# Attention scores of two heads: one product over 128 rows of the array each, or three products over 64 rows side by side

## The chip, the cores and the metric

The kernel runs on one core of a Trainium2 chip. A core has a matrix engine (TensorE; "PE" in the profile, its weight loads "PEld"), a vector engine (VectorE, "DVE"), a scalar engine (ScalarE, "ACT"), a general engine (GpSimd, "POOL") and a queue for transfers (SyncE, "SP"). They run side by side and wait for one another through semaphores. TensorE multiplies a stationary operand, which a weight load puts into the array, by a moving operand that is streamed through it; the result goes to a separate memory of eight banks, which VectorE and ScalarE read.

The metric is device microseconds of one execution, lower is better. Times are medians over several executions; the profile is of one execution, with its own time.

## What is computed

Two sequences (2048 and 512 positions, 1024 channels) go through two layers and a last RMSNorm. The first layer, which the change touches, is windowed attention with 16 query heads of width 64; every four query heads share one of 4 key and value heads:

```python
qb = q.reshape(b, nb, BLOCK, N_KV_HEADS, GROUP, HEAD_DIM)
kw = band_windows(k, nb)            # the block before, the own, the next: 384 keys
scores = jnp.einsum('bnqhgd,bnkhd->bnhgqk', qb, kw) * scale + bias
scores = jnp.where(mask, scores, -jnp.inf)
m = jnp.maximum(jnp.max(scores, axis=-1, keepdims=True), sk)
p = jnp.exp(scores - m)
p = p / (jnp.sum(p, axis=-1, keepdims=True) + jnp.exp(sk - m))
o = jnp.einsum('bnhgqk,bnkhd->bnqhgd', p, vw)
return x + (o * jax.nn.silu(gate)) @ w_out
```

`sk` is a learned logit per head, `bias` a table by distance. The second layer mixes by a two-dimensional Fourier transform, with a gate and an output projection. Everything is float32.

## The kernel before

Float32 accuracy is made of products in a shorter format (`F32R` in the code). An operand is split in two parts, "hi" (rounded) and "lo" (the rest). Most products are made of three products of parts, hi x hi, hi x lo and lo x hi: that is `matmul3` (lines 95 to 97), and each projection in the profile shows up under these three lines.

The attention layer goes through five chunks of 512 positions (`CHUNKS`: the short sequence, then four of the long one). For each chunk the keys and values of the chunk and its neighbours are projected. A key part is kept twice in `kwin`, once in partitions 0 to 63 and once in 64 to 127, for both parts, hi and lo. Then eight pairs `p` of query heads follow, each with four blocks `b` of 128 queries and two heads `j`.

- `qg_proj` projects queries and gates of a pair (128 columns, two heads of 64). Its step `evac_q` (lines 370 to 379) reads the query bank of 128 partitions, of which the first 64 are head 0 and the others head 1, and makes one tile `qab` with two halves: for head 0, hi in partitions 0 to 63 and lo in partitions 64 to 127; for head 1, hi in partitions 64 to 127 and lo in 0 to 63. Two instructions of ScalarE and two of VectorE, of 64 partitions each, do this. The queries are scaled by -1/8, so that a minimum takes the place of the maximum.
- `scores(b, j)` (line 422) makes two products over all 128 rows (line 428): the stationary operand holds hi and lo of the queries one above the other, the moving one the same part of the keys in both halves of the partitions, first hi and then lo. So two products contain all four products of parts. They run over 384 key columns, and over 256 in the first and last block of a sequence. The result stands in one of two banks, `spt`, which take turns. Then the softmax follows: VectorE adds the bias and takes the minimum (line 440), ScalarE takes the exponential with its sum (line 444), VectorE the reciprocal (line 447) and the scaling (line 450, in the first chunk also lines 453 and 456). The tile `S` has `LAG + 2` = 5 buffers.
- `transp(b, j)` transposes the probabilities on TensorE (line 467) and splits them (lines 468 and 469), `av(b)` multiplies them by the values (line 481), `out_evac(b)` adds the parts, applies the gate and splits the result for the output projection `out_proj`.

One loop over `i` sets the order: 64 steps per chunk, one for each pair of heads, block and head (`HB` lists the blocks and heads), and five more to run out. In step `i` come the scores of step `i`, the transposes of step `i - LAG` (`LAG` is 3), half of the step's share of filling work (the projections of the next pair, or the output projection), the value product of the head pair that ended two steps before (`AVLAG`), and the other half of the filling. This order is what the program hands in; a planner then orders the instructions of each engine by their priorities and its own estimate of when operands are ready, unless an order is pinned. `tc.keep_in_program_order(x)` pins `x` behind the instruction that was last handed in on its engine.

One product in the kernel does not use all of the array's rows: the bias table is looked up once at the start by a product of 33 rows and 16 columns (line 245).

Of the kernel before, what the change touches and what calls it, by code (L numbers as in the profile page):

```python
# [8 lines left out]
F32 = mybir.dt.float32  # L9
# [3 lines left out]
AF = mybir.ActivationFunctionType  # L13
ALU = mybir.AluOpType
# [4 lines left out]
P = 128  # L19
# [9 lines left out]
LAG = 3  # L29
# [10 lines left out]
def f32(ap):  # L40
    return ap.bitcast(F32)
# [3 lines left out]
def encoder(  # L45
# [3 lines left out]
    PE, ACT, DVE, POOL, SP = nc.tensor, nc.scalar, nc.vector, nc.gpsimd, nc.sync  # L49
# [85 lines left out]
    def attention_phase():  # L135

        with ExitStack() as es:
# [76 lines left out]
            ps = bank("idle")  # L214
# [40 lines left out]
            spt = []  # L255
# [98 lines left out]
            def qg_proj(c, p, hs, res, invb=None):  # L354

                steps = []
                st = {}

                def load():
                    st["q"] = load_w(c, p, f"q{c}_{p}", None if p else DVE)  # L360
                    st["g"] = load_w(c, 12 + p, f"g{c}_{p}", None if p else DVE)

                def mm(which, k):
                    if k == 0:
                        st["ps" + which] = bank(f"{which}p{c}_{p}")
                    ks = slice(k * P, (k + 1) * P)
                    w = st[which]
                    matmul3(st["ps" + which], (w[0][:, ks], w[1][:, ks]), hs[k], k == 0, k == KD - 1)

                def evac_q():  # L370
                    ps = scaled(st["psq"], invb, f"q{p}")
                    qab = ap.tile([P, 2, CH], F32R, align_bytes=LINE, tag="qab", bufs=2, name=f"qab{c}_{p}")
                    qa, qb = qab[:, 0], qab[:, 1]
                    ACT.activation(qa[0:64], ps[0:64], AF.Copy, scale=-0.125)
                    DVE.scalar_tensor_tensor(qa[64:128], ps[0:64], -0.125, f32(qa[0:64]), ALU.mult, ALU.subtract)
                    ACT.activation(qb[64:128], ps[64:128], AF.Copy, scale=-0.125)
                    DVE.scalar_tensor_tensor(qb[0:64], ps[64:128], -0.125, f32(qb[64:128]), ALU.mult, ALU.subtract)  # L377
                    res["q"] = (qa, qb)

                def evac_g():  # L380
                    ps = scaled(st["psg"], invb, f"g{p}")
                    th = ap.tile([P, CH], F32, tag="tmp", bufs=2, name=f"th{c}_{p}")
                    ACT.activation(th, ps, AF.Tanh, scale=0.5)
                    s = ap.tile([P, CH], F32, tag="s", bufs=2, name=f"s{c}_{p}")
                    DVE.scalar_tensor_tensor(s, th, 1.0, ps, ALU.add, ALU.mult)
                    res["s"] = s

                steps.append(load)
                for k in range(KD):
                    steps.append(lambda k=k: mm("q", k))  # L390
                steps.append(evac_q)
                for k in range(KD):
                    steps.append(lambda k=k: mm("g", k))
                steps.append(evac_g)
                return steps

            def attention(c, p, res, uTs):
# [21 lines left out]
                    k1 = 2 if tok + (b + 1) * P == hi_t else 3  # L419
                    return gb, k0, k1  # L420

                def scores(b, j):
                    gb, k0, k1 = span(b)
                    q = res["q"][j][:, b * P : (b + 1) * P]
                    ps = spt[nS[0] % 2]
                    nS[0] += 1
                    for part in range(2):
                        PE.matmul(  # L428
                            ps[:, 2 + k0 * P : 2 + k1 * P],
                            q,  # L430
                            kwin[g][:, part, b * P + k0 * P : b * P + k1 * P],
                            start=part == 0,
                            stop=part == 1,
                        )

                    e0, e1 = (1 + k0 * P, 386) if k1 == 3 else (0, 1 + k1 * P)
                    n = e1 - e0
                    s = ap.tile([P, 388], F32, tag="S", bufs=LAG + 2, name=f"S{c}_{p}_{b}_{j}")
                    mn, den = s[:, 386:387], s[:, 387:388]
                    DVE.tensor_tensor_reduce(  # L440
                        out=s[:, e0:e1], in0=ps[:, 1 + e0 : 1 + e1], in1=st["bias"][:, j, 386 - e1 : 386 - e0][:, ::-1],
                        scale=1.0, scalar=3.0e38, op0=ALU.add, op1=ALU.min, accum_out=mn,
                    )
                    last_exp[0] = ACT.activation(  # L444
                        s[:, e0:e1], s[:, e0:e1], AF.Exp, bias=mn, scale=-1.0, accum_out=den
                    )
                    DVE.reciprocal(den, den)  # L447
                    ks = slice(1 + k0 * P, 1 + k1 * P)
                    if c:
                        DVE.tensor_scalar(s[:, ks], s[:, ks], den, None, ALU.mult)  # L450
                    elif j:

                        ACT.activation(s[:, ks], s[:, ks], AF.Copy, scale=den)
                    else:

                        DVE.tensor_scalar(s[:, ks], s[:, ks], den, None, ALU.mult, ALU.add, accum_out=mn)
                    st[b, j] = s
# [234 lines left out]
            for c in range(len(CHUNKS)):  # L692

                if c > 1:
                    hs, halo = make_h(c, invb)
                for s in tail:
                    s()
                if c == 1:
                    hs, halo = make_h(c, invb)
                if c:  # L700
                    invb0 = kv_proj(c, hs, halo)
                else:
                    invb0 = kv_proj(c, hs, halo, first_norms, early)
                rowd, sk = bias
                uTs = []
                res = [{} for p in range(8)]
                at = [attention(c, p, res[p], uTs) for p in range(8)]
                for s in qg_proj(c, 0, hs, res[0], invb0):
                    s()
                at[0][0]()  # L710
                fill = []
                for i in range(64 + LAG + AVLAG):
                    p, n = divmod(i, 8)
                    if n == 0 and i < 64:
                        if p < 7:

                            fill = qg_proj(c, p + 1, hs, res[p + 1], invb0)
                            fill.pop(0)()
                            at[p + 1][0]()
                            if i == 0 and c == 0:  # L720

                                for s in fill[:8]:
                                    s()
                                fill = fill[8:]
                        else:
                            op = out_proj(c, uTs)
                            fill, rest, tail = op[:4], op[4:7], op[7:]
                    if c + 1 < len(CHUNKS):
                        if i == 24:
                            norm_steps = stats(c + 1)  # L730
                        if i >= 38 and i % 2 == 0 and norm_steps:
                            inv = norm_steps.pop(0)()
                        elif i == 56:
                            invb = spread(c + 1, inv)
                    if c in EXTRA and i in EXTRA[c]:
                        EXTRA[c][i]()
                    if c == len(CHUNKS) - 1 and i in AHEAD:
                        AHEAD[i]()
                    if c == 0 and i % 8 == 3 and 1 <= p < 3:
                        load_w(0, LATE[p - 1], f"late{p}", late=last_exp[0])  # L740
                    if i < 64:
                        at[p][1](*HB[n])
                    k = i - LAG
                    if 0 <= k < 64:
                        at[k // 8][2](*HB[k % 8])
                    if i < 64:
                        m = len(fill) * (n + 1) // 8 - len(fill) * n // 8
                        todo = fill[len(fill) * n // 8 :][:m]
                        for s in todo[: m // 2]:
                            s()  # L750
                    k -= AVLAG
                    if 0 <= k < 64 and k % 2 == 1:
                        b = k % 8 // 2
                        at[k // 8][3](b)
                        if b % 2 == 1:
                            at[k // 8][4](b)
                    if i < 64:
                        for s in todo[m // 2 :]:
                            s()
                    elif rest:  # L760
                        rest.pop(0)()
# [802 lines left out]
```

## Time and profile before

| what | value |
|---|---|
| median of 3 runs | 1649.08 us (1646.85 to 1652.1) |
| the profiled execution, its time | 1648.75 us |
| its span, first to last instruction | 1647.0 us |
| TensorE busy | 1628.4 us (99%), 8939 matmuls |
| VectorE busy | 1199.0 us (73%) |
| ScalarE busy | 892.7 us (54%) |
| GpSimd busy | 434.5 us (26%) |
| granted TensorE clock, mean | 0.998 |

Matmuls are pipelined: one that follows starts long before the one ahead of it has ended, so the profile's durations of single matmuls overlap. How long a matmul holds the engine is read from the distance between starts, or from the chain in order of time, where each piece lasts until the next. "Busy" counts the time in which at least one is under way. In a group of the profile, "128*128 128x384" says how many rows and columns of the array are used, and how many partitions and elements the result has. The releaser behind an arrow is inferred from semaphores.

### The profile page before, as it was taken

Reading aid. Unit: us, or ns where it says so; the run is one execution under the profiler, and the core shown is the slowest. Engines: PE = TensorE matmul, PEld = TensorE weight load, DVE = VectorE, ACT = ScalarE, POOL = GpSimd, SP = SyncE. Lnnn points to the kernel's source line nnn. Section 1 sums busy time; section 2 is a strip of 40 time slices with the busy share of each in tenths; the row PEclk is TensorE's granted clock in tenths of the full one; section 3 lists DMA queues with packets and bytes.
Section 4 is the critical chain, followed back from the end, with each engine's and each line's share of the span. In section 5 each row is a group of like instructions: output and inputs, shape, how many; then the busy total and the mean of one; then the engine's idle time right before and its main releaser. Section 6 shows DMA issues by size and latency. Waiting matters only on the chain.

```text
span 1647.0 us, 25858 instructions
## 1 busy us (share of the span) xinstructions
PE 1628.4 (99%) x8939; PEld 1401.4 (85%) x8939; DVE 1199.0 (73%) x2844; ACT 892.7 (54%) x2035; POOL 434.5 (26%) x605
## 2 busy tenths in 40 slices
PE   9999999999999999999999999999999999999998
PEld 7887888888898888988888888888888888888886
DVE  6787565888538886478884588858767667988696
ACT  6788644677326675256762466636545454343252
POOL 2454751431404322224214142121111111100010
PEclk9999999999999999999999999999999999999999
DMA  8475886665766555765648765657565469655862
GB/s 303 150 284 213 314 319 225 221 230 186 278 218 227 196 217 182 279 250 160 233 140 312 252 210 187 217 195 249 205 237 185 173 220 391 217 192 191 333 208 90
DMA packets 100637, 374.05 MB, mean 227 GB/s; under 512 B 12139, under 2 KB 22379, under 8 KB 83100
## 3 DMA queue, kind: packets, MB, share of 16 engines
q1 hardware_dynamic: 81708, 297.91, 52.2%
q0 software_dynamic: 16464, 70.30, 11.0%
q10 hardware_dynamic: 2336, 4.20, 0.7%
q8 instruction: 71, 1.16, 0.3%
q14 instruction: 58, 0.48, 0.1%
HBM read 281.10 MB, written 91.26 MB: 226 GB/s over the span
## 4 chain that ended last, share of the span: by engine, by line
PE 82%; DMA 4%; DVE 4%; POOL 3%; ACT 3%; issue 2%; SPq 0%; POOLq 0%; DVEq 0%; ACTq 0%
PE av L481 6%; PE spt L428 6%; PE pt L467 5%; PE qp L95 4%; PE qp L97 4%; PE qp L96 4%; PE op L95 4%; PE gp L95 4%; PE op L97 4%; PE gp L97 4%; PE op L96 4%; PE gp L96 4%; PE W L96 2%; PE W L97 2%; PE W L95 2%
## 5 line engine op out<-in xcount | busy, mean ns | idle before, releaser
L444 ACT ACTIVATE S<-S 128x385 f32<-128x385 f32 (+1 forms) x320 | 190.8, 596 | 63.3 <-DVE S L440 61.5
L469 DVE TENSOR_TENSOR pts<-pt,pts 128x384 fp32r<-128x384 f32 (+1 forms) x320 | 168.4, 526 | 42.0 <-ACT pts L468 39.6
L468 ACT CAST pts<-pt 128x384 fp32r<-128x384 f32 (+1 forms) x320 | 144.0, 452 | 83.4 <-PE pt L467 80.3
L440 DVE CUSTOM_DVE_ANT_0 S<-spt,b 128x385 f32<-128x385 f32 (+1 forms) x320 | 168.4, 527 | 28.2 <-PE spt L428 25.7
L428 PE MATMUL spt<-kwin,qab 128*128 128x384 f32 (+1 forms) x640 | 157.2, 327 | 1.9 <-DVE S L440 1.7
L500 POOL TENSOR_TENSOR o<-o,s 128x256 f32<-128x256 f32 x75 | 55.3, 738 | 375.0 <-DVE o L498 374.9
L467 PE MATMUL pt<-ident,S 128*128 128x128 f32 x896 | 150.7, 273 | 0.0
L428 PEld LDWEIGHTS spt<-kwin,qab 128*128 128x128 f32 x640 | 117.9, 188 | 27.9 <-DVE S L440 3.0
L95 PE MATMUL qp<-h,wq 128*128 128x512 f32 x320 | 137.5, 430 | 2.0 <-ACT wq L116 1.4
L95 PE MATMUL gp<-h,wg 128*128 128x512 f32 x320 | 137.8, 431 | 0.0
L481 PEld LDWEIGHTS av<-pts,v 128*128 128x128 f32 x896 | 126.3, 189 | 12.1 <-DVE qab L377 0.6
L481 PE MATMUL av<-pts,v 128*128 128x256 f32 x896 | 135.8, 285 | 0.3 <-DVE qab L377 0.2
L95 PE MATMUL op<-wo,uT 128*128 128x512 f32 x320 | 126.5, 397 | 1.6 <-ACT invb L173 0.9
L97 PE MATMUL qp<-h,wq 128*128 128x512 f32 x320 | 126.7, 396 | 0.2 <-POOL wq L121 0.2
L467 PEld LDWEIGHTS pt<-ident,S 128*128 128x128 f32 x896 | 113.9, 140 | 15.1 <-DVE pts L469 3.5
L96 PE MATMUL qp<-h,wq 128*128 128x512 f32 x320 | 126.2, 395 | 0.0
L97 PE MATMUL gp<-h,wg 128*128 128x512 f32 x320 | 125.9, 393 | 0.0
L96 PE MATMUL gp<-h,wg 128*128 128x512 f32 x320 | 125.7, 393 | 0.0
L96 PE MATMUL op<-wo,uT 128*128 128x512 f32 x320 | 125.7, 393 | 0.0
L97 PE MATMUL op<-wo,uT 128*128 128x512 f32 x320 | 124.7, 391 | 0.0
L450 DVE TENSOR_SCALAR S<-S 128x384 f32<-128x384 f32 (+1 forms) x256 | 118.7, 464 | 7.9
L447 DVE RECIPROCAL S<-S 128x1 f32<-128x1 f32 x320 | 51.3, 160 | 65.7 <-ACT S L444 62.7
(408 smaller groups left out, 4252.4 us busy)
## 6 DMA issues: line engine op xcount, KB each, us to landing
wo<-wsd SPq DMA_DIRECT2D x32, 1024.0 KB, 5.0
wq<-wsd SPq DMA_DIRECT2D x31, 1024.0 KB, 4.9
wg<-wsd SPq DMA_DIRECT2D x31, 1024.0 KB, 6.8
x<-x1d SPq DMA_DIRECT2D x40, 512.0 KB, 3.9
b<-b21d SPq DMA_DIRECT2D x40, 512.0 KB, 5.4
b<-rowd SPq DMA_DIRECT2D x40, 384.0 KB, 4.3
xs<-in_x_dram SPq DMA_DIRECT2D x23, 512.0 KB, 6.1
s2d<-gt POOLq DMA_DIRECT2D x40, 256.0 KB, 3.9
```

The lines of the kernel that those rows point to most:

```text
L95: PE.matmul(out, a[0], b[0], start=start, stop=False, skip_group_check=more)
L96: PE.matmul(out, a[0], b[1], start=False, stop=False, skip_group_check=more)
L97: PE.matmul(out, a[1], b[0], start=False, stop=stop, skip_group_check=more)
L428: PE.matmul(ps[:, 2 + k0 * P : 2 + k1 * P], q, kwin[g][:, part, b * P + k0 * P : b * P + k1 * P], start=part == 0, stop=part == 1,)
L440: DVE.tensor_tensor_reduce(out=s[:, e0:e1], in0=ps[:, 1 + e0 : 1 + e1], in1=st["bias"][:, j, 386 - e1 : 386 - e0][:, ::-1], scale=1.0, sca ...
L444: last_exp[0] = ACT.activation(s[:, e0:e1], s[:, e0:e1], AF.Exp, bias=mn, scale=-1.0, accum_out=den)
L450: DVE.tensor_scalar(s[:, ks], s[:, ks], den, None, ALU.mult)
L467: PE.transpose(ps[:, kb, :], s[:, 1 + kb * P : 1 + (kb + 1) * P], ident)
L468: ACT.copy(hi[:, k0:k1, j, :], ps[:, k0:k1, :])
L469: DVE.tensor_tensor(lo[:, k0:k1, j, :], ps[:, k0:k1, :], f32(hi[:, k0:k1, j, :]), ALU.subtract)
L481: PE.matmul(out, v, pt[:, kb].rearrange("p h q -> p (h q)"), start=kb == k0 and part == 0, stop=kb == k1 - 1 and part == 1,)
L500: eng.tensor_tensor(o, o, s, ALU.mult)
```

## The change

The queries of both heads now lie in one layout: `qab[:, 0]` holds hi and `qab[:, 1]` lo, each with head 0 in partitions 0 to 63 and head 1 in 64 to 127. One instruction of ScalarE and one of VectorE, of 128 partitions, make them.

`scores(b)` handles both heads of a block. It makes three products of parts per head, hi x hi, hi x lo and lo x hi, each over the 64 partitions of its head, so over 64 rows of the array; lo x lo is left out. The products of head 0 and head 1 alternate, head 0 in bank `spt[0]`, head 1 in `spt[1]`. All six are pinned in the order in which they are handed in. The softmax of both heads (`soft`, the unchanged rest of the old function) follows. In the loop `scores` is called in every other step, for both heads; transposes, value products and filling keep their steps. The buffers of `S` are 5, as before, written as a number.

```diff
                 def evac_q():
                     ps = scaled(st["psq"], invb, f"q{p}")
                     qab = ap.tile([P, 2, CH], F32R, align_bytes=LINE, tag="qab", bufs=2, name=f"qab{c}_{p}")
-                    qa, qb = qab[:, 0], qab[:, 1]
-                    ACT.activation(qa[0:64], ps[0:64], AF.Copy, scale=-0.125)
-                    DVE.scalar_tensor_tensor(qa[64:128], ps[0:64], -0.125, f32(qa[0:64]), ALU.mult, ALU.subtract)
-                    ACT.activation(qb[64:128], ps[64:128], AF.Copy, scale=-0.125)
-                    DVE.scalar_tensor_tensor(qb[0:64], ps[64:128], -0.125, f32(qb[64:128]), ALU.mult, ALU.subtract)
-                    res["q"] = (qa, qb)
+                    ACT.activation(qab[:, 0], ps, AF.Copy, scale=-0.125)
+                    DVE.scalar_tensor_tensor(qab[:, 1], ps, -0.125, f32(qab[:, 0]), ALU.mult, ALU.subtract)
+                    res["q"] = qab
...
-                def scores(b, j):
+                def scores(b):
+
                     gb, k0, k1 = span(b)
-                    q = res["q"][j][:, b * P : (b + 1) * P]
-                    ps = spt[nS[0] % 2]
-                    nS[0] += 1
-                    for part in range(2):
-                        PE.matmul(
-                            ps[:, 2 + k0 * P : 2 + k1 * P],
-                            q,
-                            kwin[g][:, part, b * P + k0 * P : b * P + k1 * P],
-                            start=part == 0,
-                            stop=part == 1,
-                        )
+                    for i, (qp, kp) in enumerate(((0, 0), (0, 1), (1, 0))):
+                        for j in range(2):
+                            rows = slice(64 * j, 64 * j + 64)
+                            tc.keep_in_program_order(PE.matmul(
+                                spt[j][:, 2 + k0 * P : 2 + k1 * P],
+                                res["q"][rows, qp, b * P : (b + 1) * P],
+                                kwin[g][rows, kp, b * P + k0 * P : b * P + k1 * P],
+                                start=i == 0,
+                                stop=i == 2,
+                            ))
+                    for j in range(2):
+                        soft(b, j)
+
+                def soft(b, j):
+                    gb, k0, k1 = span(b)
+                    ps = spt[j]
...
-                    s = ap.tile([P, 388], F32, tag="S", bufs=LAG + 2, name=f"S{c}_{p}_{b}_{j}")
+                    s = ap.tile([P, 388], F32, tag="S", bufs=5, name=f"S{c}_{p}_{b}_{j}")
...
-                    if i < 64:
-                        at[p][1](*HB[n])
+                    if i < 64 and n % 2 == 0:
+                        at[p][1](n // 2)
```

## The prediction

> **What bounds the kernel now.** I read the page first (shares, slices, chain by engine and line), then busy time by stretches, then who waits for whom on PE.
>
> ```profile
> span 1647.0 us, 25858 instructions
> PE 1628.4 (99%) x8939; PEld 1401.4 (85%) x8939; DVE 1199.0 (73%) x2844; ACT 892.7 (54%) x2035; POOL 434.5 (26%) x605
> ...
> PE 82%; DMA 4%; DVE 4%; POOL 3%; ACT 3%; issue 2%; SPq 0%; POOLq 0%; DVEq 0%; ACTq 0%
> PE av L481 6%; PE spt L428 6%; PE pt L467 5%; PE qp L95 4%; PE qp L97 4%; PE qp L96 4%; PE op L95 4%; PE gp L95 4%; PE op L97 4%; PE gp L97 4%; PE op L96 4%; PE gp L96 4%; PE W L96 2%; PE W L97 2%; PE W L95 2%
> ```
>
> TensorE is busy 99% of the span and holds 82% of the chain that ended last; the score products (L428) are 6% of it. A busy PE need not be full, so two stretches of attention come next. Columns are length, then busy time of PE, PEld, DVE, ACT, POOL, the granted clock, DMA share, GB/s.
>
> ```profile
> 254.00:458.00 204.00, 204.00 (x1131) 176.72 (x1130) 150.75 (x436) 115.69 (x296) 61.86 (x77) 1.00 0.64 225
> ...
> 662.00:866.00 204.00, 204.00 (x1173) 179.60 (x1171) 150.67 (x424) 116.34 (x288) 51.52 (x69) 1.00 0.61 212
> PE spt L428 <- DVE S L440: 1.7, 2, 1.4
> ...
> PE av L481 <- DVE qab L377: 0.2, 1, 0.2
>   PEld spt L428: 3.0, 5
> ```
>
> In attention PE has no idle time, at clock 1.00, while VectorE has 53 us of 204 free and ScalarE 88. PE waits for the evaluation of scores 1.7 us in all (plus 3.0 us ahead of weight loads, last row, from the view of L440) and for the queries 0.2 us. So any PE time that the change saves or adds there is the kernel's, and work taken from VectorE or ScalarE is worth almost nothing.
>
> **What a score product costs now.** The chain in order of time gives spacings, not the overlapping durations:
>
> ```profile
> 591.66 0.35 PE spt L428 x2
> 592.01 0.33 PE pt L467 x3
> 592.34 0.23 PE gp L95
> ...
> 596.50 0.35 PE spt L428 x2
> L428 PE MATMUL spt<-kwin,qab 128*128 128x384 f32 x512 | 131.5, 338 | 1.7 <-DVE S L440 1.7
> L428 PE MATMUL spt<-kwin,qab 128*128 128x256 f32 x128 | 25.7, 283 | 0.1
> 48.03 0.64 PE L428 MATMUL spt<-kwin,qab 128*128 128x256 f32 x4
> 48.50 0.40 PE L95 MATMUL gp<-h,wg 128*128 128x512 f32 x1
> ```
>
> Two products over 384 key columns hold PE 0.35 us, 0.175 each. The four over 256 columns run from 48.03 to 48.50, 0.118 each; 512 columns take 0.23. A pair of heads in one block now has four: 512/4 = 128 pairs at 0.70 us and 128/4 = 32 pairs at 0.47, together 104.6 us, the 6% of the chain.
>
> **Products of parts.** Each pair now issues six products in three rounds instead of four in four. No row of this trace shows two products at once in different rows of the array, so the cost is bounded: at best two side by side cost one, three rounds, 0.525 and 0.354 us; at worst six follow one another, 1.05 and 0.708. Against four, that is 128 x -0.175 + 32 x -0.118 = -26.2 us, or 128 x 0.35 + 32 x 0.236 = +52.4. Between lies a limit of weight loads: each product loads its own 128 columns, and loads stand no closer than 0.11 us below. Six in a row take 0.65: less than four products now at 384 columns, more at 256. The likeliest value I take is the best case: the streamed columns set the spacing in the rows above (0.118, 0.175, 0.23 for 256, 384, 512), and two heads stream through different rows.
>
> **The change of array shape.** The six work on 64 rows; what stands ahead and behind works on 128. The trace has one such change, the small bias product (L245: 33 rows by 16 columns, far from 128 x 128), in both directions. PE, then PEld:
>
> ```profile
> 17.25 0.39 PE L96 MATMUL kp<-h,wk 128*128 128x512 f32 x1
> 17.47 0.39 PE L97 MATMUL kp<-h,wk 128*128 128x512 f32 x1
> 17.79 1.03 PE L245 MATMUL bp<-oh,rb 33*16 33x512 f32 x2
> 18.75 0.38 PE L95 MATMUL vp<-wv,h 128*128 128x256 f32 x1
> 18.97 0.28 PE L96 MATMUL vp<-wv,h 128*128 128x256 f32 x1
> 17.25 0.19 PEld L97 LDWEIGHTS kp<-h,wk 128*128 128x128 f32 x1
> 17.79 0.11 PEld L245 LDWEIGHTS bp<-oh,rb 33*16 33x16 f32 x2 [0.35 <-issue]
> 18.75 0.19 PEld L95 LDWEIGHTS vp<-wv,h 128*128 128x128 f32 x1 [0.85 <-ACT xs L155]
> 18.86 0.19 PEld L96 LDWEIGHTS vp<-wv,h 128*128 128x128 f32 x1
> L245 PE MATMUL bp<-oh,rb x2: 589/594/600, 17.8 to 18.2; 33*16 33x512 f32 x2
> ```
>
> Normally a weight load starts with the product before it (17.25 and 17.25). At the change it does not: L97 starts at 17.47, its follower would at 17.70, yet load and product start at 17.79: 0.09 us late, and waiting for nothing shown. The two bias products end at 18.82 together, the second lasts 0.59, so it began at 18.23, 0.44 behind the first; the next could begin at 18.67 and does at 18.75, 0.08 late. Its load too starts only then, and the product behind stands 0.22 away instead of the 0.118 of 256 columns: 0.10 for the exposed load of 128 columns. (The wait for xs named there is no proof of a data wait: the release is inferred.) Into 64 rows I take 0.09 + 0.10, since the new loads have 128 columns; back 0.08 + 0.10: 0.37 us per pair. The Trainium skill (TensorEngine Tiling (Array Packing), Tiling Modes, Key Properties) states that a change of tiling mode drains the TensorE, without a price. The trace shows late starts of 0.09 and 0.08; were a drain the whole tail of a 512-column product, 0.39 - 0.23 = 0.16, the change would be 2 x (0.16 + 0.10) = 0.52 a pair by that rule and the sum below +57 instead of +33, an estimate that lies inside my forecast's own range.
>
> Bounds: at least 0, because scores to transposes changes kind of product without loss (0.35 and 0.33 above are whole spacings), and the bias product is one sample of another type and shape; at most a full latency and a full load each way, 0.39 - 0.23 + 0.19 = 0.35, or 0.70 a pair. Times 160 pairs: 0, 59.2 or 112 us. I take 59.2, from the only row that changes rows.
>
> **Order.** The six are pinned, each behind the PE instruction traced before it, where scores could earlier slip forward into a gap. In attention there is no gap, so I count 0; the wait it could lengthen is the 4.7 us for L440. Queued behind a waiting score product are transposes, projections and value products, all on PE. Both heads now fill both banks at once, and VectorE must read both before the next pair, two steps (591.66 to 596.50, 4.84 us) on. One head's softmax takes:
>
> ```profile
> 603.64 0.55 DVE L440 CUSTOM_DVE_ANT_0 S<-spt,b 128x385 f32<-128x385 f32 x1
> 604.24 0.62 ACT L444 ACTIVATE S<-S 128x385 f32<-128x385 f32 x1
> 604.98 0.16 DVE L447 RECIPROCAL S<-S 128x1 f32<-128x1 f32 x1
> 605.18 0.42 DVE L450 TENSOR_SCALAR S<-S 128x384 f32<-128x384 f32 x1
> 601.21 0.52 PE L428 MATMUL spt<-kwin,qab 128*128 128x384 f32 x2
> ```
>
> Scores begun at 601.21 are read at 603.64 to 604.19, 3.0 us on; a second head's read adds 0.55, to 3.5, or ends 4.94 us on if it stands behind the first head's whole chain (at 605.60). The first leaves 1.3 us of slack, so 0; without that cover 0.1 us on each of 160 pairs, 16 us. The transposes come three steps after the scores (1.5 x 4.84 = 7.3 us) for the first head and four for the second, against chains that end 4.4 and at most 6.4 us after them. Five score tiles remain; the sixth tile needed reuses one whose transposes stand a step earlier, so no new wait.
>
> **Queries.** Per pair of heads and chunk, four evacuations of 64 partitions become two of 128:
>
> ```profile
> L374 ACT ACTIVATE qab<-qp x40: 572/588/593, 38.5 to 1047.2; 64x512 fp32r<-64x512 f32 x40
> L375 DVE SCALAR_TENSOR_TENSOR qab<-qp,qab x40: 683/684/687, 39.1 to 1048.1; 64x512 fp32r<-64x512 f32 x40
> L376 ACT ACTIVATE qab<-qp x40: 592/593/598, 39.8 to 1049.0; 64x512 fp32r<-64x512 f32 x40
> L377 DVE SCALAR_TENSOR_TENSOR qab<-qp,qab x40: 692/693/694, 40.4 to 1049.9; 64x512 fp32r<-64x512 f32 x40
> ```
>
> If 128 partitions take as long as 64, 40 x 0.59 = 23.7 us of ScalarE and 40 x 0.69 = 27.7 of VectorE go, none on the path: PE waits for queries 0.2 us. If the time grows with partitions, nothing goes and nothing is lost. Count 0. DMAs, bias, softmax arithmetic, transposes and value products keep their number.
>
> **Sum.** -26.2 + 59.2 = +33 us. The profiled run took 1648.75 with a span of 1647.0; the median of the runs is 1649.08, 0.3 above. 1648.75 + 33 is about 1682.
>
> **Rivals.** (1) *The change of rows is free* and the heads run side by side: -26.2, so 1622.5; faster. For it: PE is the bound with no idle time, and the change from scores to transposes costs nothing. Against it: the bias product. It decides once a pair loses under 26.2/160 = 0.16 us, less than half of my 0.37. (2) *Weight loads follow one another* and the change of rows costs 0.37: the rounds take six loads, five beyond the first, already paid, then one last stream. At 384 columns 5 x 0.11 + 0.175 = 0.725 + 0.37 against 0.70, +0.395 x 128; at 256, 0.55 + 0.118 + 0.37 against 0.47, +0.568 x 32: +69, so 1717. For it: load rows never overlap by more than their tail. Against: nothing in the rows beyond that the loads shown all use the same rows of the array. The Trainium skill, in the same section, has different tiles load and multiply in parallel, which would exclude (2) and (3); no run here shows it yet. (3) *The heads don't run side by side*, so the change doesn't do what it says: +52.4 + 59.2 = +112, so 1760. No row speaks for or against. (4) *Free change, loads in line*: six at 0.11 against four, 128 x -0.04 + 32 x 0.19 = +1, so about 1650.
>
> **How the numbers follow.** Chances: my forecast 0.43; (1), with a switch under 0.16, 0.20; (2) 0.19; (3) 0.10; (4) 0.08, of which 0.05 within 0.3%, which is about what a measurement can tell from no change. Slower: 0.43 + 0.19 + 0.10 + 0.03 = 0.75; same 0.05; faster 0.20. The range leaves out (3) and the dearest switch, 0.10 to 0.15: from 1620, under (1), to 1728, over (2). The likeliest's own, with 0.25 to 0.52 us a pair for the switch (40 to 83 us), is 1662 to 1706.
>
> **What would show it.** In the profile after: L428-type products in 64 rows, starting in twos within a few hundredths of a us if side by side, rounds 0.175 apart (right) or 0.22 (rival 2) or twice 0.175 (rival 3); a first weight load that starts with its own product rather than with the one before, and the same for the first load behind the six, some 0.37 us a pair (right) or a load already early (rival 1). PE's waits for the score reads should stay under 10 us; more means that the banks are held. VectorE's busy time should fall by up to 28 us without effect. The prediction is wrong if other matmuls slip between the six (each time another change of rows, 0.37), or if the bias product's delay was a data wait.

## The result and the profile after

The changed kernel takes 1675.3 us (median of 4 runs, 1674.4 to 1676.51) against 1648.64 for the kernel before beside it: 1.0157 times as long, 95% interval 1.0143 to 1.0171. That is 26.7 us slower; 33 were forecast.

The first view is the page of the changed kernel: its span, shares and chain by line. L425 are now the score products (L428 before), L470 the transposes, L484 the value products, L443 the reading of the scores.

```profile
span 1673.8 us, 26522 instructions
## 1 busy us (share of the span) xinstructions
PE 1656.0 (99%) x9259; PEld 1353.6 (81%) x9259; DVE 1177.5 (70%) x2804; ACT 874.9 (52%) x1995; POOL 435.2 (26%) x605
...
PE pt L470 6%; PE spt L425 6%; PE av L484 6%; PE qp L95 4%; PE qp L97 4%; PE qp L96 4%; PE op L95 4%; PE gp L95 4%; PE gp L97 4%; PE gp L96 4%; PE op L96 4%; PE op L97 4%; PE fo L97 2%; PE fo L96 2%; PE fo L95 2%
```

TensorE is still busy 99% of the span; the span grew by 26.8 us and TensorE's busy time by 27.6. VectorE does 21.5 us less and ScalarE 17.8, and nobody gained by it. The score products are still 6% of the chain: three rounds in place of four did not make them cheaper. The transposes rose from 5 to 6%.

Next come PE's instructions in order of time around one pair of heads, then PEld's in the same stretch (columns: start, duration of the merged group, engine, line).

```profile
599.89 0.39 PE L96 MATMUL qp<-h,wq 128*128 128x512 f32 x1
600.12 0.40 PE L97 MATMUL qp<-h,wq 128*128 128x512 f32 x1
600.45 0.80 PE L425 MATMUL spt<-kwin,qab 64*128 64x384 f32 x6
601.17 0.55 PE L470 MATMUL pt<-ident,S 128*128 128x128 f32 x3
601.47 0.49 PE L95 MATMUL qp<-h,wq 128*128 128x512 f32 x1
```

```profile
599.89 0.19 PEld L97 LDWEIGHTS qp<-h,wq 128*128 128x128 f32 x1
600.45 0.47 PEld L425 LDWEIGHTS spt<-kwin,qab 64*128 64x128 f32 x6 [0.36 <-DVE o L501]
601.17 0.31 PEld L470 LDWEIGHTS pt<-ident,S 128*128 128x128 f32 x3 [0.25 <-ACT pts L471]
```

Read the distances of the starts. The product ahead holds PE from 600.12 to 600.45, 0.33 us instead of 0.23: 0.10 lost on the way in. The six hold it from 600.45 to 601.17, 0.72 us. Six in line at 0.175 would be 1.05, three rounds 0.525; the rest, 0.20, is the first load, now exposed, and the way out. One by one, the trace has the six starting in twos, 3 to 4 ns apart: at 600.446 and 600.450, 600.729 and 600.732, 600.906 and 600.910. The first round takes 0.28 instead of 0.18, so the exposed load is 0.10; from the last round to the transposes it is 0.26, so the way out is 0.09. The three transposes go from 601.17 to 601.47, 0.30 instead of the 0.24 that stood between 601.57 and 601.81 before (rows of the next fence, kernel before): 0.06 for their exposed load. Both first loads, at 600.45 and at 601.17, start with their own product and not with the one ahead, as a load does otherwise (599.89 and 599.89). The releasers named in the brackets are inferred: the small product of an experiment below has the same delay in a kernel of the old order.

```profile
601.57 0.49 PE L467 MATMUL pt<-ident,S 128*128 128x128 f32 x3
601.81 0.48 PE L95 MATMUL qp<-h,wq 128*128 128x512 f32 x1
```

So a pair at 384 columns loses 0.10 + (0.72 - 0.70) + 0.06 = 0.18 us. A pair at 256 columns, from the same view near the start:

```profile
48.04 0.39 PE L97 MATMUL qp<-h,wq 128*128 128x512 f32 x1
48.36 0.62 PE L425 MATMUL spt<-kwin,qab 64*128 64x256 f32 x6
48.91 0.50 PE L95 MATMUL gp<-h,wg 128*128 128x512 f32 x1
49.25 0.40 PE L96 MATMUL gp<-h,wg 128*128 128x512 f32 x1
```

Here the way in costs 0.09, the six take 0.55 against 0.47, and the 512-column product behind takes 0.34 instead of 0.23. With 0.06 behind where transposes follow, 128 x 0.18 + 32 x 0.23 = 30 us; the measured difference is 26.7. Summed over the whole of both traces, the distances from a start to the next grew by 15.3 us behind products of 512 columns, 8.8 behind transposes and 2.8 behind score products, and by nothing behind the rest together: 26.9. The first two are about what the rows give. The score products should have grown by 128 x 0.02 + 32 x 0.08 = 5.1 us by the rows; most of the 3 to 4 us lies there, since the kernel before has longer pauses between its score products than the changed one. PE's waits for the reading of scores are not the cause of the loss:

```profile
PE spt L425 <- DVE S L443: 1.8, 3, 0.8
```

```profile
  DVE S L443: 5.3, 8
```

The first row is from who waited for whom on PE, the second from the view of L425, for PE and its weight loads together: 5.3 us against 4.7 before.

### The profile page after: what moved, and what is told of

It reads as the page before. It is cut to its first block, busy times and chain, and to the rows that moved or that the text cites. A ratio compares the mean times of both kernels' runs of the same rounds, so it can differ in the third digit from the quotient of the medians.

```text
span 1673.8 us, 26522 instructions
## 1 busy us (share of the span) xinstructions
PE 1656.0 (99%) x9259; PEld 1353.6 (81%) x9259; DVE 1177.5 (70%) x2804; ACT 874.9 (52%) x1995; POOL 435.2 (26%) x605
## 4 chain that ended last, share of the span: by engine, by line
PE 85%; DVE 4%; ACT 3%; DMA 3%; issue 2%; POOL 2%; SPq 0%; DVEq 0%; POOLq 0%; ACTq 0%
PE pt L470 6%; PE spt L425 6%; PE av L484 6%; PE qp L95 4%; PE qp L97 4%; PE qp L96 4%; PE op L95 4%; PE gp L95 4%; PE gp L97 4%; PE gp L96 4%; PE op L96 4%; PE op L97 4%; PE fo L97 2%; PE fo L96 2%; PE fo L95 2%
## 5 line engine op out<-in xcount | busy, mean ns | idle before, releaser
L443 DVE CUSTOM_DVE_ANT_0 S<-spt,b 128x385 f32<-128x385 f32 (+1 forms) x320 | 157.2, 528 | 35.6 <-PE spt L425 35.0
L470 PE MATMUL pt<-ident,S 128*128 128x128 f32 x896 | 158.4, 282 | 0.0
L470 PEld LDWEIGHTS pt<-ident,S 128*128 128x128 f32 x896 | 104.9, 140 | 57.0 <-issue 15.9
L484 PEld LDWEIGHTS av<-pts,v 128*128 128x128 f32 x896 | 125.9, 189 | 11.4
L484 PE MATMUL av<-pts,v 128*128 128x256 f32 x896 | 134.8, 284 | 0.0
L425 PE MATMUL spt<-kwin,qab 64*128 64x384 f32 (+1 forms) x960 | 122.6, 358 | 1.8 <-DVE S L443 1.8
L425 PEld LDWEIGHTS spt<-kwin,qab 64*128 64x128 f32 x960 | 74.5, 185 | 59.8 <-issue 16.5
L95 PE MATMUL fo<-wo,tTu 128*128 128x512 f32 x192 | 75.6, 394 | 0.0
```

Of the source, the lines that this page charges most:

```text
L95: PE.matmul(out, a[0], b[0], start=start, stop=False, skip_group_check=more)
L425: tc.keep_in_program_order(PE.matmul(spt[j][:, 2 + k0 * P : 2 + k1 * P], res["q"][rows, qp, b * P : (b + 1) * P], kwin[g][rows, kp, b * P ...
L443: DVE.tensor_tensor_reduce(out=s[:, e0:e1], in0=ps[:, 1 + e0 : 1 + e1], in1=st["bias"][:, j, 386 - e1 : 386 - e0][:, ::-1], scale=1.0, sca ...
L470: PE.transpose(ps[:, kb, :], s[:, 1 + kb * P : 1 + (kb + 1) * P], ident)
L484: PE.matmul(out, v, pt[:, kb].rearrange("p h q -> p (h q)"), start=kb == k0 and part == 0, stop=kb == k1 - 1 and part == 1,)
```

## The experiments

My theory: a pair pays for the change of array rows, in and out, more than the third of the product time that it saves. Rivals: the new order and the pins lose the time; the products don't run side by side; the loss lies in something else that came with the change.

**Order alone.** The changed kernel's order (both heads in one step, pinned), with the products over 128 rows:

```diff
+ (evac_q as in the kernel before)
-                    for i, (qp, kp) in enumerate(((0, 0), (0, 1), (1, 0))):
-                        for j in range(2):
+                    for j in range(2):
+                        for part in range(2):
...
+                                res["q"][j][:, b * P : (b + 1) * P],
+                                kwin[g][:, part, b * P + k0 * P : b * P + k1 * P],
```

> Both heads of a block are scored in the same step and pinned, as in the changed kernel, but with the query layout and the two products over 128 rows per head of the kernel before. Theory (all of the loss is the change of array rows): order and pins cost nothing, so the time of before, 1648.6 us, within 0.3% (1644 to 1654), and the six transitions per pair show no late weight load. Rival (the new order, both banks held at once and the pins lose the time): clearly above before, up to 1675 us, with more than 10 us of PE waits for the reading of the scores.

Measured: 1651.17 us, 1.0009 times before, interval 1.0 to 1.0018. The order costs nothing, or at most 0.2%. In the chain in order of time of this kernel, four products take what two pairs of two took, and the transposes behind them take 0.33 as before:

```profile
603.11 0.70 PE spt L427 x4
603.81 0.33 PE pt L472 x3
```

**A fourth round.** The changed kernel with lo x lo:

```diff
-                    for i, (qp, kp) in enumerate(((0, 0), (0, 1), (1, 0))):
+                    for i, (qp, kp) in enumerate(((0, 0), (0, 1), (1, 0), (1, 1))):
...
-                                stop=i == 2,
+                                stop=i == 3,
```

> The changed kernel with the fourth product of parts (lo x lo) put back, so four rounds of two products. Theory (two heads side by side cost one round): 128 x 0.175 + 32 x 0.118 = 26.2 us more than the changed kernel's 1675.3, so 1701.5 us. Rival (the heads don't run side by side, each product costs its own stream): 52.4 us more, 1728 us.

Measured: 1702.71 us, 27.4 above the changed kernel's 1675.3; 26.2 was expected for a round side by side, 52.4 for products in line. The chain shows the eight products of a pair, and first the six of the changed kernel:

```profile
600.52 0.72 PE spt L425 x6
601.24 0.48 PE pt L470 x3
```

```profile
609.11 0.89 PE spt L425 x8
```

Two more products cost 0.17 us, one stream of 384 columns: the heads do run side by side. The transposes behind the six stand at 0.48 in this view instead of 0.33. The chain shares a pair's loss out in another way than the starts do, but its sum is the same: 0.72 - 0.70 and 0.48 - 0.33 are 0.17, against 0.18 by the starts.

**Head after head.** The same six products, but neighbours in the program use the same rows:

```diff
-                    for i, (qp, kp) in enumerate(((0, 0), (0, 1), (1, 0))):
-                        for j in range(2):
+                    for j in range(2):
+                        for i, (qp, kp) in enumerate(((0, 0), (0, 1), (1, 0))):
```

> The changed kernel with the same six products in another order: the three of head 0, then the three of head 1, so that neighbours use the same 64 rows. Theory (products run side by side only when neighbours in the order use different rows): head 0's third and head 1's first pair up, five rounds instead of three, 128 x 0.35 + 32 x 0.236 = 52.4 us more than 1675.3, so 1728 us. Rival (TensorE pairs them whatever their order): 1675 us. Rival (no pairing at the border either): six rounds, 1754 us.

Measured: 1684.87 us, 9.6 above the changed kernel and far from 1728: my expectation was wrong. PE in order of time:

```profile
605.76 0.40 PE L97 MATMUL qp<-h,wq 128*128 128x512 f32 x1
606.09 0.80 PE L425 MATMUL spt<-kwin,qab 64*128 64x384 f32 x6
606.82 0.55 PE L470 MATMUL pt<-ident,S 128*128 128x128 f32 x3
```

The six still take 0.73 us, so three rounds, starting in twos: TensorE starts head 1's products beside head 0's though head 0's others stand ahead of them in the program. (The trace doesn't name a product's head; that the order is the program's rests on the pins. It fits that both products of the last round now raise their semaphore by more than one, where in the changed kernel the last one raises it by one.) The Trainium skill (TensorE: Matmul & The Clock Gate, Part 3, The mechanism) says that matmuls are not reordered; this trace differs, and it decides. At most 0.01 a pair, 1.6 us, of the 9.6 lies in the pairs themselves. The view of who waited for whom has PE waits of 5.0 us in the transposes for VectorE, and the changed kernel has no such row of 0.2 us or more:

```profile
PE pt L470 <- DVE pts L472: 5.0, 14, 1.2
```

And busy time by stretches (clock third from the right) has 4.6 us at half clock, which cost about half of that, 2.3 us; the changed kernel, second, ran there at clock 1.00. Why this order brings such waits stays open, and so does the rest.

```profile
181.00:185.60 4.60, 4.60 (x11) 3.60 (x12) 2.59 (x9) 3.10 (x9) 2.58 (x5) 0.50 0.97 386
```

```profile
181.00:185.60 4.60, 4.60 (x27) 3.58 (x28) 3.90 (x16) 3.32 (x10) 3.14 (x5) 1.00 0.99 362
```

**The change of rows by itself.** The kernel before, with a small product ahead of each pair's scores, whose result the scores overwrite:

```diff
+                    if j == 0:
+                        PE.matmul(
+                            ps[:128, 2 + k0 * P : 18 + k0 * P],
+                            q[:64, :128],
+                            kwin[g][:64, 0, b * P + k0 * P : b * P + k0 * P + 16],
+                            start=True,
+                            stop=True,
+                        )
                     for part in range(2):
```

The control has 128 in place of 64; the third has no `if`, so one small product for each head; the fourth has 32 in place of 128.

> The kernel before with one small product over 64 rows (128 query columns loaded, 16 key columns streamed) ahead of each pair's first score product; its result is overwritten. 160 changes of rows into and out of, nothing else. Theory (a change empties the array and exposes the next weight load): 0.096 + 0.105 in, 0.02 for the stream, 0.087 + 0.105 out = 0.41 us x 160 = 66 us, so about 1715 us. Rival (a change of rows costs nothing, the small product costs its weight load alone): 0.11 x 160 = 17.6, about 1666 us.

> The control for the small product: the same one over 128 rows, so the rows never change. Both theories: it holds TensorE for one weight load, 0.11 us x 160 = 17.6 us, so about 1666 us.

> The small product over 64 rows ahead of each head's scores, so 320 changes of rows. Theory (each change costs the same): twice what one per pair costs, 132 us, about 1780 us. Rival (part of the cost is hidden once, or is a wait that occurs only once per pair): less than twice.

> The small product over 64 rows with only 32 query columns loaded, one per pair. Theory (emptying, 0.096 and 0.087, plus an exposed load that goes with the number of columns, 0.105 for 128): the load on the way in shrinks to about 0.03, so 0.34 us x 160 = 54 us, about 1703 us, 12 less than with 128 columns. Rival (a fixed price of the change, whatever is loaded): the same time as with 128 columns.

| small product | time, us | above before (1647.95) | each |
|---|---|---|---|
| 64 rows, 128 columns, 160 times | 1706.74 | 58.8 | 0.367 |
| 128 rows, 128 columns, 160 times | 1667.78 | 19.8 | 0.124 |
| 64 rows, 128 columns, 320 times | 1766.76 | 118.8 | 0.371 |
| 64 rows, 32 columns, 160 times | 1696.79 | 48.8 | 0.305 |

The ratios to before are 1.0352 (1.0335 to 1.0369), 1.0122 (1.0106 to 1.0139), 1.0717 (1.0699 to 1.0734) and 1.0298 (1.0281 to 1.0315). With 64 rows the same small product costs three times what it costs with 128, 0.24 us more, and twice as many changes cost twice as much. PE around one small product with 64 rows and 128 columns, then with 32 columns:

```profile
599.93 0.40 PE L97 MATMUL qp<-h,wq 128*128 128x512 f32 x1
600.26 0.27 PE L428 MATMUL spt<-kwin,qab 64*128 64x16 f32 x1
600.46 0.62 PE L436 MATMUL spt<-kwin,qab 128*128 128x384 f32 x2
600.92 0.49 PE L475 MATMUL pt<-ident,S 128*128 128x128 f32 x3
```

```profile
599.75 0.40 PE L97 MATMUL gp<-h,wg 128*128 128x512 f32 x1
600.08 0.19 PE L428 MATMUL spt<-kwin,qab 64*32 64x16 f32 x1
600.20 0.62 PE L436 MATMUL spt<-kwin,qab 128*128 128x384 f32 x2
```

In: 0.33 instead of 0.23, in both. The small product: 0.20 with 128 columns loaded, 0.12 with 32, so the load on the way in goes with its columns and the rest doesn't. Behind: two score products hold PE 0.46 (600.46 to 600.92) instead of 0.36. Of the price, one part is a fixed emptying each way and one the exposed load. The expected 1715, 1780 and 1703 were 6 to 13 us too high: each change was taken at what one stretch showed, and the average is lower.

**Fewer changes.** The changed kernel with the products of two blocks together, and of four; the blocks share the two banks:

```diff
+                    if b % 2 == 0:
+                        for bb in (b, b + 1):
...
+                            (the six products of block bb)
```

> The products of two blocks are issued together in every fourth step, so that the rows change 80 times instead of 160; the two blocks share the two banks, so the softmax of the first block reads the scores of the second. The number of products is that of the changed kernel. Theory (each pair pays 0.096 + 0.105 us on the way in and 0.087 + 0.055 on the way out, read from the changed kernel's starts): 80 x 0.343 = 27.4 us less than 1675.3, so 1648 us. Rival (the loss lies in the products themselves or in the order, not in the change of rows): 1675 us.

> As the kernel with 80 changes of rows, but the products of all four blocks of a pair of heads go out together in every eighth step: 40 changes. The four blocks share the two banks, so the softmax of the first three reads the scores of the fourth. Theory (the loss goes with the number of changes): by the starts 120 x 0.343 = 41.2 us less than 1675.3, 1634 us; by what halving gave (22.4 us for 80 changes, 0.28 each) 33.6 less, 1642 us; both below the kernel before. Rival (halving removed the loss by something else, such as fewer waits for banks, and the rest is not the change of rows): about 1653 us, as with 80 changes.

Measured: 1652.87 us with 80 changes (1.0029 times before, 1.0017 to 1.004) and 1644.1 with 40 (0.9969, 0.9958 to 0.9979). Against 1675.3, that is 22.4 us for 80 changes less, 0.28 each, and 31.2 for 120 less, 0.26 each; by the starts, 27.4 and 41.2 had been expected. The rival's 1653 for 40 changes falls. The number of products is the same in all three. The chain with 80 changes shows twelve products and the transposes behind:

```profile
603.59 1.25 PE spt L428 x12
604.84 0.48 PE pt L473 x3
```

Two groups of six took 1.44; one group of twelve takes 1.25. The second six add 1.25 - 0.72 = 0.53 us, three rounds of 0.175 and nothing more: within a visit, products over 64 rows have no price of their own. So the three products do save time, and between 80 and 40 changes they begin to pay. These two kernels show a time and are not to be used: each block's scores overwrite those of the block before it in the group. To keep them, each block would need two banks of its own, and of eight banks six hold the other products.

**The queries.** The changed kernel with its two evacuations of 128 partitions cut into four of 64:

```diff
-                    ACT.activation(qab[:, 0], ps, AF.Copy, scale=-0.125)
+                    for rows in (slice(0, 64), slice(64, 128)):
+                        ACT.activation(qab[rows, 0], ps[rows], AF.Copy, scale=-0.125)
...
```

> The changed kernel with its two query evacuations of 128 partitions cut into four of 64 partitions, as many as before. Theory (work taken from ScalarE and VectorE is worth nothing, TensorE has no idle time): 1675 us, within 0.3%, while ScalarE's busy time rises by about 24 us and VectorE's by about 27. Rival (the shorter evacuation hides a larger loss): above 1680 us.

Measured: 1675.29 us, 1.0163 times before (1.0149 to 1.0177): no difference from the changed kernel. The groups by line, changed kernel first, then the four parts:

```profile
L374 DVE SCALAR_TENSOR_TENSOR qab<-qp,qab 128x512 fp32r<-128x512 f32 x40 | 27.7, 691 | 32.3 <-ACT qab L373 32.2
L373 ACT ACTIVATE qab<-qp 128x512 fp32r<-128x512 f32 x40 | 23.9, 599 | 38.9 <-PE qp L97 29.1 <-DVE qp L270 9.5
```

```profile
L375 DVE SCALAR_TENSOR_TENSOR qab<-qp,qab 64x512 fp32r<-64x512 f32 x80 | 55.1, 688 | 39.0 <-ACT qab L374 37.5
L374 ACT ACTIVATE qab<-qp 64x512 fp32r<-64x512 f32 x80 | 47.4, 593 | 57.6 <-PE qp L97 29.7 <-DVE qab L375 17.7 <-DVE qp L270 9.8
```

One instruction takes the same for 64 and 128 partitions; 27.4 us of VectorE and 23.5 of ScalarE are worth nothing here.

## Why the prediction was right

**The bound.** PE had no idle time in attention, so its extra work showed up whole: 27.6 us more busy time, 26.7 us more time. The relief of VectorE and ScalarE was worth 0, as said.

**Products of parts.** Counted at -26.2 us for three rounds side by side. The fourth round cost 27.4, and eight products stand 0.17 above six. Right; rival (3), products in line, falls, and rival (2), loads in line, too: the six loads end 0.47 us after the first began, while six in line at 0.11 would need 5 x 0.11 + 0.19 = 0.74.

**The change of rows.** Counted at 0.09 + 0.10 in and 0.08 + 0.10 out, 0.37 a pair, from one small product at the start of the kernel of before. Measured in the changed kernel: 0.10 late on the way in; 0.20 for the first load and the emptying on the way out together, inside the 0.72, where 0.18 was counted; 0.06 for the load behind: 0.36 by the rows in view. The term that was mis-sized is the last: the exposed load ahead of transposes costs 0.06, not 0.10, which is 160 x 0.04 = 6.4 us. Where a 512-column product follows, it is 0.11, as counted. That 6.4 is just the distance between 33 and 26.7 is chance: the other terms came out up to 0.01 higher each, which by the rows gives 30, and the rest lies in the pauses of the kernel before. Spread over all pairs, the change cost (26.2 + 26.7) / 160 = 0.33; taking visits away saved a little less, 0.26 to 0.28 each, and the difference isn't traced. That one product of 33 rows and 16 columns gave the price of 64 rows and 128 columns so closely was partly luck; it was one sample. The rule of the Trainium skill that a change of mode drains the TensorE (TensorEngine Tiling (Array Packing), Key Properties) agrees with the 0.10 on the way in, which stood at 0.33 instead of 0.23 with 128 and with 32 columns loaded alike; a drain of the whole tail, 0.16, is not what the rows show.

**Rival (1), a free change**, falls with the small product: 0.367 with 64 rows against 0.124 with 128. Its turning point, 0.16 us a pair, was borne out: half as many changes are half of 0.33 a pair, and the kernel was within 0.3% of before; with a quarter it was faster.

**Order.** Counted at 0: 0.09% in the experiment, with an interval from 0 to 0.18%. The waits for banks went from 4.7 to 5.3 us, under the 10 that I had named.

## What to carry to other kernels

Two products over 64 rows each ran side by side at the price of one here, but only the group as a whole counts: each visit to another array shape cost 0.26 to 0.33 us, as much as one and a half to two streams of 384 columns. Before such a change, count visits and the streams that each saves; one saved stream of 0.175 us per visit was not enough, and groups of two visits merged into one (twelve products) were about the point of balance. Look in the trace of before for any product of another shape, however small: its late weight loads gave the price.

## What had not been expected of the hardware

TensorE itself pairs products that use different rows, as far as the pinned order was kept: with head 0's three products ahead of head 1's in the program, the six still took 0.73 us, three rounds. A scalar or vector instruction over 512 elements took the same for 64 and for 128 partitions (593 and 599 ns, 688 and 691 ns), so merging two halves halved the cost.
